# The first MLP's shift vectors: one group moved to VectorE, one held and multiplied on TensorE inside the norm's chain

## The chip, the cores and the metric

The kernel runs on one core of one Trainium2 chip. The metric is the device time of one execution in microseconds (us), as a median of several runs. Below, PE is TensorE's matmul queue, DVE is VectorE, ACT is ScalarE, POOL is GpSimd, and SP is SyncE, whose queue issues nearly all the loads.

## The reference

A trunk of two layers on 256 positions of width 2048. Layer 0 mixes with a causal convolution module (pw1, a gate, a depthwise convolution, a LayerNorm, pw2), layer 1 with a Mamba-2 mixer. An MLP follows each mixer. Every sublayer is normed, and scaled, shifted and gated by vectors that come from one conditioning vector c:

```python
sc = jax.nn.silu(c)
for i in range(DEPTH):
    mod = (sc @ w_mod[i] + b_mod[i])[:, None, :]
    sh1, sc1, g1, sh2, sc2, g2 = jnp.split(mod, 6, axis=-1)
    u = rmsnorm(h, norm_mix_g[i]) * (1 + sc1) + sh1
    ...
    h = h + g1 * mix
    u = rmsnorm(h, norm_mlp_g[i]) * (1 + sc2) + sh2
    h = h + g2 * sq_relu_mlp(u, mlp_w1[i], mlp_w2[i])
return rmsnorm(h, final_norm_g)
```

`sc @ w_mod[i]` is a matrix of 2048 x 12288 times one vector: much to load, little to compute. The change is about sh2, the shift of the first MLP, called SH2 in the code.

## The kernel before

**Modulation columns.** Each of the six vectors of a layer has 16 tiles of 128 outputs. A tile ("column" below) is loaded as 128 x 2048 from `wmT` (1 MB) into a buffer `wm` (two of them) or `hid` (four). Four columns form a group, whose 4 results per partition lie in one small tile `mod<layer><vector><group>`: mod033 is SH2's group 3, mod043 is SC2's, mod023 is G1's. `gemv` multiplies a column in one of two ways. On VectorE it is one instruction (L293) that multiplies the tile by silu(c) and sums it. For groups in `PE_GROUPS` it is four matmuls on TensorE (L284), each of 32 columns, into a PSUM bank from the pool `ms` (two banks); after a group's fourth column ACT copies the bank (L290), and `columns` transposes the copy on TensorE (L305) and reduces it on VectorE (L307). Then GpSimd adds the bias (L321), and for scale vectors applies the norm's weight (L323, L324). All of SH2, groups 0 to 3, is in `PE_GROUPS` before.

**The order of the columns.** `EARLY` lists the columns that are worked between the start of pw1 and the opening of the first MLP; `pump(n)` takes the next n. How many are taken beside each weight tile is written out in tables: `RATE_PW1` for the last four blocks of pw1, `BETWEEN` in the LayerNorm, `RATE_PW2` for the 16 tiles of pw2, `RATE_OPEN` for the 12 tiles of the first MLP's opening.

**The weights.** Each weight tile is 1 MB (four k-tiles of 512 columns), in one of three buffers `w32` (the profile writes `w`). It is split in two halves into a high part `wh` (ACT, L362) and a low part `wl` (VectorE, L364), three buffers of each, so a half is cast as soon as TensorE is done with the half three before it. A tile then takes 48 matmuls (L377): high by high, high by low, low by high. In a name as the profile prints it, `u` is the activation with high and low parts, and `mm` a PSUM bank of the products.

**The stages that matter**, in time order. pw2 runs as `outer` over its blocks 0 to 2 (twelve tiles) and `block` for block 3 (four tiles). Block 3's evacuation (L928) and squares (L567) end the residual. The norm's chain follows: `rstd_cols` sums the squares over partitions on TensorE (L541), ACT takes the root (L546), VectorE the reciprocal (L547) and the diagonal (L516), and TensorE broadcasts it (L521). Then VectorE and ACT make u for the first quarter (`modulate`: nrm L575, high part L505, low part L506), and `outer` starts the first MLP with three blocks together (twelve tiles), quarter by quarter: u for quarter g needs mod03g and mod04g. TensorE's waits in that chain are filled by `turn_over` (L529), matmuls of constants whose result nobody reads, so many as `FILL` says.

**What sets the order on a queue.** A scheduler places each engine's instructions from the program's order, priorities (`high_priority`) and explicit marks (`issue_after`). Loads keep their program order on SP (`stream`, L348). On each engine the instructions then run strictly in their order, each waiting for its semaphores.

Of the kernel before, what the change touches and what calls it, by code (L numbers as in the profile page):

```python
# [15 lines left out]
P = 128  # L16
# [27 lines left out]

RATE_PW1 = [1, 1, 1, 1, 1, 2, 1, 1, 1, 2, 1, 1, 1, 1, 0, 0]
BETWEEN = 5
RATE_PW2 = [1] * 12 + [2, 1, 2, 1]
RATE_OPEN = [1] * 9 + [0] * 3  # L50
RATE_MLP = spread(80, 116) + [0] * 50
RATE_OUT = spread(24, 32)
RATE_LAST = spread(8, 12)
# [12 lines left out]

EARLY = [(0, s, 4 * g + i) for s, g in ((G1, 0), (G1, 1), (G1, 2), (SC2, 0), (SH2, 0), (SH2, 1)) for i in range(4)]
_te = [(0, SH2, 5 + i) for i in range(11)]  # L70
_ve = [(0, G1, 12 + i) for i in range(4)] + [(0, SC2, 4 + i) for i in range(12)]
_mix = _ve[:1]
for _i in range(5):
    _mix += [_te[2 * _i], _ve[1 + _i], _te[2 * _i + 1]]
EARLY = EARLY[:-3] + _mix + _te[10:] + _ve[6:]


PE_GROUPS = {(0, SH2, g) for g in range(4)}
WAIT = 3


# [99 lines left out]
class Trunk:  # L181
    def __init__(self, ctx, nc, tc, a):
        self.nc, self.tc, self.a = nc, tc, a
        pool = lambda n, **kw: ctx.enter_context(tc.tile_pool(name=n, **kw))
        self.one = pool("one", bufs=1)
        self.big = pool("big", bufs=1)
        self.wp = pool("wp", bufs=1)
        self.tp = pool("tp", bufs=2)
        self.mm = pool("mm", bufs=6, space=PSUM)
        self.ms = pool("ms", bufs=2, space=PSUM)  # L190
        self.dr = pool("dr", bufs=1, space=DRAM)
        self.uid = 0
        self.jobs = []
        self.todo = []
        self.ahead = AHEAD
        self.ring, self.rings = 0, ("wm", "hid", "hid")
        self.mod = {}
        self.rows_left = []
        self.spare = 1
        self.act = None  # L200
        self.side = self.mm, "mm"
        self.prologue()
# [61 lines left out]
                                          name=f"mod{layer}{seg}{kg}")  # L264
        return self.mod[key]

    def gemv(self, layer, seg, ct, parts=((0, 4),)):

        nc = self.nc
        self.ring += 1  # L270
        tag = self.rings[self.ring % len(self.rings)]
        w = self.b(tag, [P, D], bufs=4 if tag == "hid" else 2)
        self.stream(w, self.a["wmT"][layer, seg, ct])
        g, i = divmod(ct, 4)
        m = self.mod_tile(layer, seg, g)
        if (layer, seg, g) in PE_GROUPS:
# [185 lines left out]
    def outer(self, srcs, make, evac, pump, there=()):  # L462


        banks = [[self.bank(self.mm, "mm") for _ in range(2)] for _ in srcs]
        self.turn_over(banks[0][0][:, :P], FILL[4] if there else FILL[3], self.pe)
        there = list(there)
        for g in range(4):
            x = make(g)
# [41 lines left out]
    def rstd_bcast(self, sums, n):  # L511

        nc = self.nc
        r = self.rstd_cols(sums, n, FILL[1])
        dg = self.t("diag", [P, 2, P], bufs=1)
        self.dg = nc.vector.tensor_tensor(  # L516
            out=dg, in0=self.ident.rearrange("p (o k) -> p o k", o=1).broadcast_to([P, 2, P]),
            in1=r.rearrange("p (q o) -> p q o", o=1).broadcast_to([P, 2, P]), op=ALU.mult).ins
        ps = self.bank(self.ms, "ms")[:, :T]
        self.turn_over(ps[:, :P], FILL[2], self.pe)  # L520
        self.pe = nc.tensor.matmul(ps, lhsT=self.ones, rhs=dg.rearrange("p q k -> p (q k)"), start=True,  # L521
                                   stop=True).ins
        return ps
# [9 lines left out]
    def rstd_cols(self, sums, n, fill=0):  # L533
# [1 line left out]
        nc = self.nc  # L535
        ps = self.bank(self.ms, "ms")
        if fill:
            self.turn_over(ps[:, :P], fill, self.pe)
        for i, s in enumerate(sums):
            for q in range(2):  # L540
                ins = nc.tensor.matmul(ps[:, q:q + 1], lhsT=s[:, q * P:(q + 1) * P], rhs=self.ones[:, :1],  # L541
# [40 lines left out]
    def conformer(self):  # L582
# [310 lines left out]
        def make(g):  # L893
            if g:
                normed(g)
            if g == 3:
# [3 lines left out]
                for b in range(4):  # L900
# [7 lines left out]
        into = [self.into_h(res, b, gate) for b in range(4)]  # L908
        self.outer([a["pw2"][b] for b in range(3)], make, lambda b, j, parts: into[b](j, parts), pump,
                   there=[(there[0], [half]), (there[1], ()), (there[2], ())])  # L910
        self.block(a["pw2"][3], v, into[3], pump=pump, single=True)
        return res["ss"]


# [498 lines left out]
```

## Time and profile before

| | us |
|---|---|
| median of 3 runs | 2572.73 (2571.45 to 2573.01) |
| the profiled execution's own time | 2573.06 |
| its span, first to last instruction | 2571.3 |
| conformer up to the first product of pw2 | 0 to 313.43 |
| pw2 | 313.43 to 421.03 |
| the norm's chain | 421.03 to 427.59 |
| the first MLP's opening (12 weight tiles) | 427.59 to 497.67 |

The span is what the profile's rows cover; 1.8 us of the execution lie outside it. In a row of a timeline or of the chain stand the start, the length, the engine, the name, the line and a count. One fp32 matmul of the kernel leaves two records of L284, L305, L529 or L541, so four such matmuls show as x8; the products L377 leave one each.

### The profile page before, as it was taken

How to read it: one execution, taken by the hardware profiler on the slowest of the kernel's cores; microseconds unless marked ns; L12 is line 12 of the kernel's file. 1: busy time of each engine (PE TensorE's matmuls, PEld its weight loads, DVE VectorE, ACT ScalarE, POOL GpSimd, SP SyncE). 2: the span in 40 equal slices, each digit the busy share in tenths (PEclk: the TensorE clock that was granted, in tenths of full speed). 3: DMA queues.
4: the chain of work that ended last, by engine and by line, in shares of the span. 5: the costliest groups of instructions: out<-in, count | busy, mean ns of one | idle time of the engine just before them, and what ended most of it. 6: DMA issues, size and time to landing. Idle time of an engine off the chain costs nothing.

```text
span 2571.3 us, 37102 instructions
## 1 busy us (share of the span) xinstructions
PE 2531.0 (98%) x14771; PEld 2181.7 (85%) x14771; DVE 1907.8 (74%) x2460; ACT 1312.3 (51%) x2012; POOL 149.5 (6%) x212
## 2 busy tenths in 40 slices
PE   6999999999999999999999999999999999999998
PEld 5888789988888888888888888888998888888886
DVE  6569567977878878888877777898985565565565
ACT  2068454544434434447767777744454444443443
POOL 0011001000000000000000000000001101101000
PEclk8999999999999999999999999999999999999999
DMA  9998698788888888866555555678765555555553
GB/s 403 368 328 308 252 350 310 283 325 330 313 313 336 310 309 339 313 234 222 198 185 176 174 195 185 240 308 327 297 250 191 197 183 193 197 183 194 196 185 143
DMA packets 94895, 664.85 MB, mean 259 GB/s; under 512 B 10977, under 2 KB 10977, under 8 KB 16769
## 3 DMA queue, kind: packets, MB, share of 16 engines
q1 hardware_dynamic: 89138, 643.87, 67.7%
q0 software_dynamic: 5152, 16.97, 2.3%
q8 instruction: 115, 1.88, 0.3%
q10 hardware_dynamic: 432, 1.66, 0.2%
q14 instruction: 58, 0.48, 0.1%
HBM read 657.02 MB, written 2.20 MB: 256 GB/s over the span
## 4 chain that ended last, share of the span: by engine, by line
PE 94%; DMA 3%; DVE 2%; ACT 1%; issue 0%; POOL 0%; ACTq 0%; SPq 0%; DVEq 0%; POOLq 0%
PE mm L393 48%; PE mm L377 11%; PE mm L447 8%; PE mm L446 8%; PE mm L448 8%; PE mm L743 6%; DMA hid<-wmT 2%; PE mm L689 1%; PE ms L1325 1%; PE ms L743 1%; DMA wm<-wmT 1%; PE ms L284 0%; DVE wl L364 0%; PE ms L541 0%; DVE hid L293 0%
## 5 line engine op out<-in xcount | busy, mean ns | idle before, releaser
L364 DVE TENSOR_TENSOR wl<-w,wh 128x1024 fp32r<-128x1024 f32 x768 | 940.9, 1228 | 487.5 <-ACT wh L362 482.6
L362 ACT CAST wh<-w 128x1024 fp32r<-128x1024 f32 x768 | 806.7, 1051 | 947.4 <-PE mm L393 476.0
L393 PE MATMUL mm<-u,wh 128*128 128x512 f32 x3136 | 994.3, 398 | 0.2 <-ACT wh L362 0.2
L393 PEld LDWEIGHTS mm<-u,wl 128*128 128x128 f32 x3136 | 587.6, 188 | 138.7 <-DVE wl L364 1.3
L393 PE MATMUL mm<-u,wl 128*128 128x256 f32 x3136 | 617.9, 279 | 0.6 <-DVE wl L364 0.6
L393 PEld LDWEIGHTS mm<-u,wh 128*128 128x128 f32 x3136 | 479.9, 189 | 7.7 <-issue 4.3
L446 PE MATMUL mm<-wh,hid 128*128 128x512 f32 x896 | 350.7, 391 | 0.0
L448 PE MATMUL mm<-wh,hid 128*128 128x512 f32 x896 | 348.7, 389 | 0.0
L447 PE MATMUL mm<-wl,hid 128*128 128x512 f32 x896 | 348.7, 389 | 0.0
L293 DVE SCALAR_TENSOR_TENSOR wm<-wm,scb 128x2048 f32<-128x2048 f32 x132 | 301.5, 2284 | 16.9 <-DMA wm<-wmT 16.9
L377 PE MATMUL mm<-u,wh 128*128 128x256 f32 x1408 | 256.0, 284 | 1.6 <-ACT u L505 0.7
L377 PEld LDWEIGHTS mm<-u,wh 128*128 128x128 f32 x1408 | 219.3, 192 | 8.6 <-issue 3.4
L743 PE MATMUL mm<-u,w 128*128 128x256 f32 x864 | 193.3, 385 | 19.6 <-ACT u L617 19.6
L743 PEld LDWEIGHTS mm<-u,w 128*128 128x128 f32 x864 | 165.6, 193 | 46.6 <-ACT u L617 20.8
L377 PE MATMUL mm<-u,wl 128*128 128x256 f32 x704 | 198.6, 283 | 0.0
L446 PEld LDWEIGHTS mm<-wh,hid 128*128 128x128 f32 x896 | 168.2, 188 | 35.6 <-issue 1.0
L447 PEld LDWEIGHTS mm<-wl,hid 128*128 128x128 f32 x896 | 168.2, 188 | 35.2 <-issue 0.5
L448 PEld LDWEIGHTS mm<-wh,hid 128*128 128x128 f32 x896 | 168.2, 188 | 35.1
L393 PE MATMUL mm<-hid,wh 128*128 128x512 f32 x448 | 141.8, 397 | 0.0
L377 PEld LDWEIGHTS mm<-u,wl 128*128 128x128 f32 x704 | 134.7, 192 | 1.7 <-DVE wl L364 0.8
L293 DVE SCALAR_TENSOR_TENSOR hid<-hid,scb 128x2048 f32<-128x2048 f32 x44 | 100.4, 2284 | 43.0 <-DMA hid<-wmT 35.6
L321 POOL TENSOR_TENSOR mod<-mod,par 128x4 f32<-128x4 f32 x46 | 38.0, 826 | 1118.4 <-DVE wm L293 907.8
(263 smaller groups left out, 2029.7 us busy)
## 6 DMA issues: line engine op xcount, KB each, us to landing
w<-w SPq DMA_DIRECT2D x256, 1024.0 KB, 4.9
wm<-wmT SPq DMA_DIRECT2D x139, 1024.0 KB, 7.4
w<-win SPq DMA_DIRECT2D x80, 1024.0 KB, 4.9
hid<-wmT SPq DMA_DIRECT2D x53, 1024.0 KB, 11.1
w<-pw SPq DMA_DIRECT2D x46, 1024.0 KB, 6.8
w<-wout SPq DMA_DIRECT2D x32, 1024.0 KB, 7.2
acc<-ac_d POOLq DMA_DIRECT2D x16, 512.0 KB, 7.5
xpad<-u POOLq DMA_DIRECT2D x24, 131.5 KB, 8.4
```

The lines of the kernel that those rows point to most:

```text
L293: self.sum = nc.vector.scalar_tensor_tensor(out=w, in0=w, scalar=1.0, in1=self.scb, op0=ALU.mult, op1=ALU.mult, accum_out=m[:, i:i + 1]).ins
L321: nc.gpsimd.tensor_tensor(out=m, in0=m, in1=b, op=ALU.add)
L362: nc.scalar.copy(out=wh, in_=w[:, s, :])
L364: nc.vector.tensor_tensor(out=wl, in0=w[:, s, :], in1=wh.bitcast(F32), op=ALU.subtract)
L377: self.pe = self.nc.tensor.matmul(out, lhsT=lhsT, rhs=rhs, skip_group_check=True, **kw).ins
L393: self.pe = self.nc.tensor.matmul(out, lhsT=lhsT, rhs=rhs, start=start and not lows, stop=stop and bool(lows), skip_group_check=True).ins
L446: mm(banks[q], lhsT=hi, rhs=wh[:, k, :], start=g == 0 and t == 0, stop=False)
L447: mm(banks[q], lhsT=hi, rhs=wl[:, k, :], start=False, stop=False)
L448: mm(banks[q], lhsT=lo, rhs=wh[:, k, :], start=False, stop=g == 3 and t == 3)
L689: self.pe = nc.tensor.matmul(o[32 * c:32 * c + 32, :], lhsT=w[:, k, 32 * c:32 * c + 32], rhs=r[:, c, k:k + T], start=k == 0, stop=k == 7, ...
L743: self.pe = nc.tensor.matmul(o, lhsT=w[:, t, j * P:(j + 1) * P], rhs=u[g][:, t, :], start=g == 0 and t == 0 and j < 2, stop=g == 3 and t == 3,
L1325: nc.tensor.matmul(py[64 * f:64 * f + 64, jj * T + q * Q:jj * T + (q + 1) * Q], lhsT=xd[q][:, r, :], rhs=sco[q][:, r, :], start=True, stop ...
```

## The change

It does four things.

- Group 3 of SH2 leaves `PE_GROUPS`: its four columns are now multiplied on VectorE, last of all of `EARLY`.
- Group 2 of SH2 leaves `EARLY`. Its columns (`HELD`) are loaded beside the last two tiles of pw2 and wait in their buffers; `turn` then takes one of them wherever the norm's chain had fillers: one ahead of the sums, one ahead of the broadcast, two ahead of the MLP's products.
- The order of `EARLY` and the rates change. Two columns of G1 are taken beside the last two tiles of pw1 (`RATE_PW1` ends on 1, 1 instead of 0, 0). pw2 takes 13 columns and loads the four held, where it took 18; the opening takes 8 where it took 9.
- `gemv` can be handed a tile that is loaded already; the loading is now `fetch`.

In the changed file the lines of the same code stand 16 to 25 lower: L300 for L284, L321 for L305, L522 for L505, L523 for L506, L538 for L521, L546 for L529, L558 for L541, L592 for L575, L309 for L293, L378 and L380 for L362 and L364, L364 for L348.

```diff
-RATE_PW1 = [1, 1, 1, 1, 1, 2, 1, 1, 1, 2, 1, 1, 1, 1, 0, 0]
+RATE_PW1 = [1, 1, 1, 1, 1, 2, 1, 1, 1, 2, 1, 1, 1, 1, 1, 1]
-RATE_PW2 = [1] * 12 + [2, 1, 2, 1]
-RATE_OPEN = [1] * 9 + [0] * 3
+RATE_PW2 = [1] * 13 + [0] * 3
+RATE_OPEN = [1] * 8 + [0] * 4
...
-EARLY = [(0, s, 4 * g + i) for s, g in ((G1, 0), (G1, 1), (G1, 2), (SC2, 0), (SH2, 0), (SH2, 1)) for i in range(4)]
-_te = [(0, SH2, 5 + i) for i in range(11)]
-_ve = [(0, G1, 12 + i) for i in range(4)] + [(0, SC2, 4 + i) for i in range(12)]
-_mix = _ve[:1]
-for _i in range(5):
-    _mix += [_te[2 * _i], _ve[1 + _i], _te[2 * _i + 1]]
-EARLY = EARLY[:-3] + _mix + _te[10:] + _ve[6:]
-PE_GROUPS = {(0, SH2, g) for g in range(4)}
+EARLY = [(0, s, 4 * g + i) for s, g in ((G1, 0), (G1, 1), (G1, 2), (SC2, 0)) for i in range(4)]
+_te = [(0, SH2, i) for i in range(8)]
+_ve = [(0, s, i) for s, i0 in ((G1, 12), (SC2, 4), (SH2, 12)) for i in range(i0, NT)]
+EARLY += _ve[:2] + _te[:5]
+for _i in range(3):
+    EARLY += [_te[5 + _i], _ve[2 + _i]]
+EARLY += _ve[5:]
+HELD = [(0, SH2, 8 + i) for i in range(4)]
+PE_GROUPS = {(0, SH2, g) for g in range(3)}
...
+    def turn(self, out, n):
+        if self.held:
+            key, w = self.held.pop(0)
+            with self.tc.issue_after(self.pe):
+                self.gemv(*key, w=w)
+        else:
+            self.pe = self.turn_over(out, n, self.pe)
...
-        self.turn_over(banks[0][0][:, :P], FILL[4] if there else FILL[3], self.pe)
+        for _ in range(len(self.held) or 1):
+            self.turn(banks[0][0][:, :P], FILL[4] if there else FILL[3])
...
-        self.turn_over(ps[:, :P], FILL[2], self.pe)
+        self.turn(ps[:, :P], FILL[2])
...
-            self.turn_over(ps[:, :P], fill, self.pe)
+            self.turn(ps[:, :P], fill)
...
-        self.block(a["pw2"][3], v, into[3], pump=pump, single=True)
+        def last(g):
+            if g > 1:
+                for key in HELD[2 * g - 4:2 * g - 2]:
+                    self.held.append((key, self.fetch(*key)))
+            return next(rate)
+        self.block(a["pw2"][3], v, into[3], pump=last, single=True)
```

What this does to the queues, at three places. First TensorE in pw2, with the products between the rows left out. Before, the columns are:

```order
L284 MATMUL ms_1939<-hid_2016,scol 32x512
...
L284 MATMUL ms_1939<-hid_2016,scol 32x512 x3
...
L284 MATMUL ms_1939<-wm_2160,scol 32x512 x4
...
L284 MATMUL ms_1939<-hid_2224,scol 32x512 x4
...
L284 MATMUL ms_2369<-wm_2366,scol 32x512 x4
...
L284 MATMUL ms_2369<-hid_2432,scol 32x512 x4
...
L284 MATMUL ms_2369<-wm_2605,scol 32x512 x4
...
L284 MATMUL ms_2369<-hid_2683,scol 32x512 x4
...
L284 MATMUL ms_2850<-wm_2847,scol 32x512 x4
L284 MATMUL ms_2850<-hid_2855,scol 32x512 x4
...
L284 MATMUL ms_2850<-wm_2986,scol 32x512 x4
L284 MATMUL ms_2850<-hid_2992,scol 32x512 x4
```

In the changed kernel, with the transposes (L321) of the two groups that are done there:

```order
L300 MATMUL ms_1946<-hid_1967,scol 32x512 x4
...
L300 MATMUL ms_1946<-hid_2084,scol 32x512 x4
L321 MATMUL ms_1918<-ident,t_266_1941 128x128 x4
...
L300 MATMUL ms_1946<-wm_2231,scol 32x512 x4
...
L321 MATMUL ms_1946<-ident,t_298_2237 128x128 x4
```

Eleven columns have become three; the first of them now stands behind eight products of the stage instead of 32.

Second, TensorE in the norm's chain, from the last product of pw2 to the first of the MLP. Before:

```order
L377 MATMUL mm_2844<-u_2562,wl_3066 128x256
L529 MATMUL ms_3131<-scb,ones 128x128 x3
L541 MATMUL ms_3131<-ones,ssum_2656 128x1 x2
L541 MATMUL ms_3131<-ones,sq_3111 128x1 x2
L541 MATMUL ms_3131<-ones,sq_3120 128x1 x2
L541 MATMUL ms_3131<-ones,sq_3129 128x1 x2
L529 MATMUL ms_3148<-scb,ones 128x128 x5
L521 MATMUL ms_3148<-diag_3146,ones 128x256
L529 MATMUL mm_3156<-scb,ones 128x128 x6
```

After:

```order
L393 MATMUL mm_2838<-u_2564,wl_3034 128x256
L300 MATMUL ms_3101<-wm_2963,scol 32x512 x4
L558 MATMUL ms_3099<-ones,ssum_2656 128x1 x2
L558 MATMUL ms_3099<-ones,sq_3079 128x1 x2
L558 MATMUL ms_3099<-ones,sq_3088 128x1 x2
L558 MATMUL ms_3099<-ones,sq_3097 128x1 x2
L300 MATMUL ms_3101<-hid_2965,scol 32x512 x4
L538 MATMUL ms_3119<-diag_3117,ones 128x256
L300 MATMUL ms_3101<-hid_3025,scol 32x512 x4
L300 MATMUL ms_3101<-wm_3027,scol 32x512 x4
```

Each run of fillers has become one held column, the last run two. They write the bank ms_3101, which is neither that of the sums nor that of the broadcast.

Third, ACT in the MLP's opening, where u of the fourth quarter is made. The casts (wh) belong, from the top, to the eighth tile (w_468, in the changed kernel w_467), the ninth and the first of the fourth quarter. Before:

```order
L362 CAST wh_3669<-w_468_3660 128x1024
L362 CAST wh_3729<-w_474_3721 128x1024
L362 CAST wh_3733<-w_474_3721 128x1024
L362 CAST wh_3804<-w_485_3802 128x1024
L505 ACTIVATE u_3785<-nrm_3786,mod_2849 128x256
L362 CAST wh_3808<-w_485_3802 128x1024
```

After:

```order
L378 CAST wh_3637<-w_467_3631 128x1024
L378 CAST wh_3641<-w_467_3631 128x1024
L522 ACTIVATE u_3751<-nrm_3752,mod_3434 128x256
L522 ACTIVATE u_3751<-nrm_3756,mod_3434 128x256
L378 CAST wh_3695<-w_473_3693 128x1024
L378 CAST wh_3699<-w_473_3693 128x1024
L522 ACTIVATE u_3751<-nrm_3760,mod_3434 128x256
```

VectorE's rows for the same place, after the change:

```order
L309 SCALAR_TENSOR_TENSOR hid_3572,mod_3434<-hid_3572,scb 128x2048
L592 SCALAR_TENSOR_TENSOR nrm_3752<-h_78,mod_3163,ms_3119 128x256
L592 SCALAR_TENSOR_TENSOR nrm_3756<-h_78,mod_3163,ms_3119 128x256
L380 TENSOR_TENSOR wl_3638<-w_467_3631,wh_3637 128x1024
L380 TENSOR_TENSOR wl_3642<-w_467_3631,wh_3641 128x1024
L309 SCALAR_TENSOR_TENSOR hid_3633,mod_3434<-hid_3633,scb 128x2048
L523 SCALAR_TENSOR_TENSOR u_3751<-nrm_3752,mod_3434,u_3751 128x256
```

mod_3434 is mod033: its last column (L309, the second of the two) stands behind the split of the eighth tile, and the two u that read it stand on ACT ahead of the ninth tile's casts, where before both halves of that tile and one of the next were cast first.

More of the change, by code (lines that the diff above doesn't have):

```diff
@@ L198, in __init__ @@
         self.rows_left = []
+        self.held = []
         self.spare = 1
@@ L265, in mod_tile, with fetch @@
         return self.mod[key]
-    def gemv(self, layer, seg, ct, parts=((0, 4),)):
-        nc = self.nc
+    def fetch(self, layer, seg, ct):
         self.ring += 1
@@ L273, in gemv @@
         self.stream(w, self.a["wmT"][layer, seg, ct])
+        return w
+    def turn(self, out, n):
[5 more added lines that the diff above has]
+            self.pe = self.turn_over(out, n, self.pe)
+    def gemv(self, layer, seg, ct, parts=((0, 4),), w=None):
+        nc = self.nc
+        w = self.fetch(layer, seg, ct) if w is None else w
         g, i = divmod(ct, 4)
```

## The prediction

> **What bounds the kernel now.** I read the first part of the page, then the table of stages, then the chain of work that ended last inside the stretch that the change touches.
>
> ```profile
> span 2571.3 us, 37102 instructions
> PE 2531.0 (98%) x14771; PEld 2181.7 (85%) x14771; DVE 1907.8 (74%) x2460; ACT 1312.3 (51%) x2012; POOL 149.5 (6%) x212
> PE 94%; DMA 3%; DVE 2%; ACT 1%; issue 0%; POOL 0%; ACTq 0%; SPq 0%; DVEq 0%; POOLq 0%
> ```
>
> TensorE (PE) works in 98% of the span and holds 94% of the chain, so a microsecond taken off PE's own queue can be one off the end, as long as nothing else is late there. The average doesn't say where; the stages do. I cut the stretch at the first product of pw2 (313.43), at the first filler of the norm (421.03), at the first product of the first MLP (427.59) and at the end of that MLP's opening (497.67); the first 100 us stand beside them for the DMA, and the end of pw1 (260 to 313.43) for the two columns that move there.
>
> ```profile
> core 0: us, PE busy (x) PEld busy (x) DVE busy (x) ACT busy (x) POOL busy (x), PEclk, DMA share, GB/s
> 0.00:100.00 100.00, 77.11 (x304) 62.04 (x305) 63.11 (x63) 18.39 (x39) 6.33 (x52) 0.90 1.00 409
> 260.00:313.43 53.43, 53.13 (x471) 38.10 (x469) 26.70 (x43) 22.56 (x51) 6.26 (x12) 1.00 0.67 246
> 313.43:421.03 107.60, 107.60 (x870) 96.34 (x871) 76.45 (x98) 54.80 (x86) 2.78 (x5) 1.00 0.90 346
> 421.03:427.59 6.56, 5.50 (x47) 5.18 (x45) 4.14 (x8) 3.37 (x7) 0.00 (x0) 1.00 0.30 105
> 427.59:497.67 70.08, 70.08 (x581) 69.89 (x582) 64.88 (x88) 35.85 (x56) 12.27 (x10) 1.00 0.79 296
> ```
>
> In pw2 PE is busy 107.60 of 107.60 us at full clock, VectorE (DVE) 76.45: whatever leaves PE there is gained. In the norm PE sits in a short chain. In the opening PE is full again, but VectorE is too, nearly: 64.88 of 70.08. That is where the change may have to pay.
>
> **Step 1: pw2 loses eight columns on PE.** "Column" is one 128x2048 tile of a modulation vector. Rows of the chain, then two groups of the same stretch:
>
> ```profile
> 317.97 0.98 PE ms L284 x2
> ...
> 321.53 0.99 PE ms L284 x6
> ...
> 327.99 0.44 PE ms L305 x4
> ...
> 353.82 0.99 PE ms L284 x8
> 354.81 5.95 PE mm L377 x48
> ...
> 361.75 0.59 PE ms L305 x4
> ...
> 393.49 1.85 PE ms L284 x16
> ...
> 401.29 0.44 PE ms L305 x4
> 401.73 5.75 PE mm L377 x48
> ...
> L284 PE MATMUL ms<-hid,scol 128*32 128x512 f32 x48 | 7.4, 600 | 0.0
> ...
> L284 PE MATMUL ms<-wm,scol 128*32 128x512 f32 x40 | 5.3, 604 | 0.0
> ```
>
> A column leaves eight records (L284 x8), so x48 and x40 are 11 columns: six alone at 0.99, two pairs at 1.85, one in two pieces at 0.98 and 0.99. That makes 5.94 + 3.70 + 1.97 = 11.6 us. A weight tile of 48 products takes 5.75 undisturbed and 5.95 behind a column, so each of the ten interruptions drags another 0.20: 2.0 us. Three transposes (L305) are 0.44 + 0.59 + 0.44 = 1.5. Together 15.1. As a cross-check, 16 tiles x 5.75 = 92.0, and 107.6 - 92.0 = 15.6; the 0.5 between the two is PE waiting at the start of the stage, and I leave it. After the change the same stage has three lone columns, 3 x 1.19 = 3.6, and two transposes, 1.0: 4.6 us. The rows therefore give 15.1 - 4.6 = **10.5 us**, and I book **10.0**. The half microsecond is kept back because VectorE gets ten columns here instead of seven.
>
> That is hidden only while VectorE keeps splitting the weights in time:
>
> ```profile
> L364 DVE TENSOR_TENSOR wl<-w,wh 128x1024 fp32r<-128x1024 f32 x32 | 38.9, 1222 | 27.2 <-ACT wh L362 27.1
> ...
> L362 ACT CAST wh<-w 128x1024 fp32r<-128x1024 f32 x32 | 33.3, 1045 | 39.1 <-PE mm L377 39.0
> ...
> L293 DVE SCALAR_TENSOR_TENSOR hid<-hid,scb 128x2048 f32<-128x2048 f32 x6 | 13.7, 2282 | 0.0
> ```
>
> A column on VectorE is 2.28 us, so three more are 6.8. VectorE's idle time there is 107.6 - 76.5 = 31.1; the stage gets 10 us shorter, which leaves about 14 us of idle in 97.6. In time order, the cast of a half tile starts when PE gives up the half three before it, that is two halves or 5.75 us before it is wanted; cast 1.05 and split 1.22 leave 3.5 us. One column (2.28) fits in that, two in a row (4.56) would be 1.1 late. In pw2 the new order always has a split between two columns, so I cost nothing more.
>
> The two G1 columns that move ahead of pw2 cost VectorE 4.6 us at the end of pw1, where it works 26.70 of 53.43, and their transfers pass SP's queue there, between pw1's last tiles and the tap tiles, at a DMA share of 0.67. I book nothing; the bounds are 0 and +2.3, one column that holds up a sum in front of the lifts.
>
> In the DMA, pw2 now moves 346 GB/s x 107.6 = 37.2 MB. It loses one column (17 for 18), so 36.2 MB in 97.6 us: 371 GB/s. The first 100 us ran at 409 with share 1.00, so the queue has room by this trace. The Trainium skill speaks against it: "DMA: Bandwidth & Descriptors", section "Where 436 GB/s comes from", takes about 358 GB/s as a core's share of HBM when both cores of a pair load, and says that this side binds for loads. By that figure the stage would last 101 us and the step would give 6.5 instead of 10; the 409 of the first row differs from it, and since one core runs here the row decides.
>
> **Step 2: the norm's chain with columns for fillers.**
>
> ```profile
> 420.87 0.83 PE L529 MATMUL ms<-scb,ones 128*128 128x128 f32 x6
> 421.54 0.50 PE L541 MATMUL ms<-ones,ssum 128*128 128x1 f32 x4
> 421.90 1.48 PE L541 MATMUL ms<-ones,sq 128*128 128x1 f32 x12
> 423.73 1.38 PE L529 MATMUL ms<-scb,ones 128*128 128x128 f32 x10 [0.35 <-ACT rcol L546]
> 424.95 0.60 PE L521 MATMUL ms<-diag,ones 128*128 128x256 f32 x2
> 425.39 1.50 PE L529 MATMUL mm<-scb,ones 128*128 128x128 f32 x12
> ...
> 423.91 0.04 DVE diag L516
> 423.95 0.31 issue
> 424.25 2.35 DVE wl L364 x2
> 426.61 0.40 DVE nrm L575
> 427.03 0.52 ACT u L505
> 427.59 6.29 PE mm L377 x50
> ```
>
> Now: fillers 0.67, sums 1.70, fillers 1.22, the broadcast 0.44, fillers, and a wait of 0.71 for the first u. The first fillers stand in front of the sums, so a column there (0.99) makes everything behind 0.32 later: diag is ready at 3.5 us into the chain instead of 3.2. The second column writes another bank, needs no wait for rcol, and ends at 0.99 + 1.70 + 0.99 = 3.7; the broadcast starts there, where before it started at 3.9 (424.95). On VectorE one of the two splits that kept nrm waiting (2.35 for both) now stands ahead of the reciprocal, in time that VectorE has free; so nrm comes at about 5.0 instead of 5.6, and u is there at 6.0. PE's own work is 3.7 + 0.44 + 1.85 for the last two columns + 0.20 = 6.2. The chain is then 6.2 against 6.56: I book **-0.3**. Bounds: -0.4, and +0.6 if four columns (3.96) simply replace 3.39 us of fillers end to end. So PE does a whole group in time that it filled before; the copy (L290) of that group goes to ACT between the second and the third u, with the half tile's 2.9 us of products to hide it.
>
> **Step 3: the opening waits for the fourth group.** One transposition more or less stays the same (one before, one after). VectorE has 8 columns for 9. But the last of them now belongs to SH2's group 3, and u of the fourth quarter needs its sum:
>
> ```profile
> 428.37 0.87 DVE L575 SCALAR_TENSOR_TENSOR nrm<-h,mod,ms 128x256 f32<-128x256 f32 x2
> ...
> 428.88 0.91 ACT L505 ACTIVATE u<-nrm,mod 128x256 fp32r<-128x256 f32 x2 [0.94 <-DVE nrm L575]
> ...
> 429.43 0.88 DVE L506 SCALAR_TENSOR_TENSOR u<-nrm,mod,u 128x256 fp32r<-128x256 f32 x2 [0.19 <-ACT u L505]
> ...
> 474.52 1.12 POOL L321 TENSOR_TENSOR mod<-mod,par 128x4 f32<-128x4 f32 x1 [16.17 <-DVE hid L293]
> ```
>
> On ACT the first two u of that quarter now stand ahead of the cast of the ninth tile's first half (half 16); before, they stood behind it. Counting from the first product, with 2.88 us a half and 0.44 for the transposes, half 16 is wanted at 46.5. The cast of half 14 ends at 36.1; VectorE then finishes the u of the quarter before (to 36.6), a column (2.28), two nrm (0.87) and two splits (2.35): 42.1. The last column ends at 44.4, GpSimd's addition (1.12) at 45.5, two u on ACT (0.91) at 46.4, the cast at 47.4 and the split at 48.6. PE's first product of that half waits 0.9; its third, which needs the split, would come at 47.8 and waits 0.8 more. Laid end to end like this the rows overstate a little: I book **+1.5**. Bounds: 0, since the order before met waits for the same quarter with PE full, and +3.5, a column and a split later still (2.28 + 1.22).
>
> **The sum.** -10.0 - 0.3 + 1.5 = -8.8. The profiled execution took 2573.06, so 2564.3; the median before is 0.33 lower than that execution, so **2564.0**. Behind the opening PE is full, and every queue has the order that it had, so I let the 8.8 reach the end.
>
> **Rivals.**
> A, transfers pace pw2. For it: share 0.90 already, and 371 GB/s wanted. Against: 409 in the first row. If the stage stays at its 346, it lasts 36.2 / 0.346 = 104.6 and gives 3.0: about 2571. Chance 0.08. (By the 358 of the Trainium skill's page above it would be 2567.5.)
> B, the held columns don't do what is meant: they land late, or the chain takes them in full. The last one is issued right behind the last tile of pw2, whose buffer comes free some 2.5 tiles (14 us) before the stage ends, and hid lands with a median of 9.2 us:
>
> ```profile
> hid<-wmT SPq DMA_DIRECT2D x12, 1024.0 KB, 9.2
> ```
>
> Against it is that margin of 5. If it happened, the chain would be 2 to 4 us longer: 2566 to 2568. Chance 0.08.
> C, VectorE becomes the bound of the opening and the fourth group costs two columns rather than a wait: +4 instead of +1.5, 2566.5 to 2568. 64.88 of 70.08 busy speaks for it, one column fewer against. Chance 0.08.
> D, slower: in pw2 every column on VectorE pushes the next split behind PE's need by its whole 2.28. Ten of them are 22.8, less the 10.0: about 2586. It decides from the point where VectorE's wait for the casts (27.1 us over 32 splits) is used up; the sum above leaves 14. Chance 0.04.
> The forecast, 2562 to 2566, has 0.72.
>
> **How the numbers follow.** 2572.73 - 0.2% is 2567.6, and a measurement of this kernel tells no less than that from no change. Faster by more: the forecast, and some two thirds of B and C and a third of A: 0.85. Within 0.2%: the rest of A, B and C: 0.11. Slower: D, 0.04. The range: at the low end 10.5 with a chain at -0.4 and no wait in the opening, 2561.8, rounded to 2561.5; at the high end B and C and the better half of A, 2568.5.
>
> **What would show it.** Right: pw2 at about 97.5 us with PE full and three columns of eight records; the norm at 6.2 to 6.6 with four; a wait of PE of 1 to 2 us for a split some 46 us into the opening, behind u of the fourth quarter; everything later shifted alike. Wrong: PE idle in pw2 behind L364 (D) or casts waiting for DMA (A), a chain over 7 us (B), more than 3 us of idle in the opening (C). I should also be wrong if the stretch before 313 grew through the two moved columns.

## The result, and the profile after

| | us |
|---|---|
| before, median of 4 runs | 2572.87 (2571.45 to 2574.26) |
| changed, median of 4 runs | 2561.74 (2561.14 to 2562.01) |
| ratio, with its 95% interval | 0.996 (0.9948 to 0.9971) |
| forecast | 2564.0 (2561.5 to 2568.5) |

The changed kernel is 11.1 us faster; the forecast was 8.8. First the page's head and the table of stages of the changed kernel, cut at the same events as before: the first product of pw2, the first matmul behind its last product, the first product of the MLP, and the first product behind its opening.

```profile
span 2559.8 us, 36983 instructions
PE 2518.8 (98%) x14707; PEld 2175.6 (85%) x14707; DVE 1916.5 (75%) x2467; ACT 1312.7 (51%) x2011; POOL 146.9 (6%) x212
...
core 0: us, PE busy (x) PEld busy (x) DVE busy (x) ACT busy (x) POOL busy (x), PEclk, DMA share, GB/s
260.00:311.64 51.64, 50.83 (x459) 36.49 (x458) 28.43 (x41) 22.71 (x51) 6.27 (x12) 1.00 0.83 299
311.64:408.57 96.93, 96.93 (x801) 93.72 (x801) 81.22 (x102) 52.46 (x83) 7.48 (x10) 1.00 0.89 348
408.57:415.07 6.50, 6.39 (x52) 2.89 (x51) 4.72 (x9) 3.69 (x7) 0.00 (x0) 1.00 0.79 272
415.07:485.63 70.56, 69.94 (x584) 69.74 (x581) 62.98 (x84) 36.30 (x56) 4.72 (x5) 1.00 0.74 280
```

The kernel before, cut exactly at the same events (the prediction's cuts lie 0.16 later at the chain and 0.17 later at the end of the opening):

```profile
313.43:420.87 107.44, 107.44 (x868) 96.18 (x869) 76.45 (x98) 54.65 (x85) 2.78 (x5) 1.00 0.90 346
420.87:427.59 6.72, 5.66 (x48) 5.34 (x46) 4.14 (x8) 3.52 (x7) 0.00 (x0) 1.00 0.31 113
427.59:497.50 69.91, 69.91 (x580) 69.72 (x581) 64.71 (x86) 35.76 (x55) 12.27 (x10) 1.00 0.79 296
```

| stage | before | after | moved | booked |
|---|---|---|---|---|
| up to the first product of pw2 | 313.43 | 311.64 | -1.79 | 0 |
| pw2 | 107.44 | 96.93 | -10.51 | -10.0 |
| the norm's chain | 6.72 | 6.50 | -0.22 | -0.3 |
| the MLP's opening | 69.91 | 70.56 | +0.65 | +1.5 |
| all behind it, to the last product | 2061.94 | 2062.33 | +0.39 | 0 |

TensorE is busy 96.93 of 96.93 us in pw2, with three columns where there were eleven, and VectorE's 81.22 still leaves it 15.7 idle. The last row is the same TensorE instructions in the same order in both; over the fourteen profiles of this study that stretch takes 2060.8 to 2062.3 in eleven and 2063.8 to 2065.9 in three, and nothing is read from it.

The first row needs a look of its own, since the two programs are the same up to that point but for two columns near its end. Windows of 3.41 us around TensorE's wait for the third quarter of u in pw1 (the kernel before, then the changed one; PEclk is the granted clock):

```profile
94.55:97.96 3.41, 0.84 (x5) 0.48 (x4) 2.56 (x4) 0.99 (x3) 0.20 (x1) 1.00 1.02 423
97.96:101.37 3.41, 3.41 (x10) 2.69 (x10) 3.41 (x4) 0.82 (x2) 0.00 (x0) 0.50 1.01 420
```

```profile
95.02:98.43 3.41, 1.75 (x8) 1.52 (x9) 2.56 (x5) 1.82 (x4) 0.20 (x1) 1.00 1.02 423
98.43:101.84 3.41, 3.41 (x18) 3.00 (x17) 3.41 (x3) 0.00 (x0) 0.00 (x0) 1.00 1.01 420
```

In the kernel before, TensorE worked 0.84 of 3.41 us in one window, and in the next it ran at half clock: 10 products instead of 18, so 1.7 us lost. In the changed kernel the same wait fell across two windows, TensorE worked 1.75 us in the emptier one, and the clock stayed. Of the -1.79, then, -1.7 is this window, -0.70 an earlier start of that quarter (96.68 for 97.38), and +0.58 a wait further on, for a DMA in front of a convolution of pw1, that this execution of the kernel before does not have:

```profile
277.81 3.67 PE L706 MATMUL mm<-xpad,acc 128*32 128x256 f32 x64 [0.51 <-DMA xpad<-u]
```

Whether any of the three belongs to the change is what part of the experiments is for.

### The profile page after: what moved, and what is told of

Read it like the earlier page. It is cut to its first block, busy times and chain, and to the rows that moved or that the text cites. A ratio compares the mean times of both kernels' runs of the same rounds, so it can differ in the third digit from the quotient of the medians.

```text
span 2559.8 us, 36983 instructions
## 1 busy us (share of the span) xinstructions
PE 2518.8 (98%) x14707; PEld 2175.6 (85%) x14707; DVE 1916.5 (75%) x2467; ACT 1312.7 (51%) x2011; POOL 146.9 (6%) x212
## 5 line engine op out<-in xcount | busy, mean ns | idle before, releaser
L380 DVE TENSOR_TENSOR wl<-w,wh 128x1024 fp32r<-128x1024 f32 x768 | 940.9, 1229 | 472.6 <-ACT wh L378 468.2
L378 ACT CAST wh<-w 128x1024 fp32r<-128x1024 f32 x768 | 808.2, 1053 | 935.4 <-PE mm L409 478.5
L309 DVE SCALAR_TENSOR_TENSOR wm<-wm,scb 128x2048 f32<-128x2048 f32 x133 | 303.9, 2285 | 17.9 <-DMA wm<-wmT 17.9
L393 PE MATMUL mm<-u,wh 128*128 128x256 f32 x1408 | 254.7, 284 | 0.9 <-DVE u L523 0.6
L393 PEld LDWEIGHTS mm<-u,wh 128*128 128x128 f32 x1408 | 219.2, 192 | 4.0 <-ACT u L519 1.3
L393 PE MATMUL mm<-u,wl 128*128 128x256 f32 x704 | 198.0, 283 | 0.6 <-DVE wl L380 0.6
L309 DVE SCALAR_TENSOR_TENSOR hid<-hid,scb 128x2048 f32<-128x2048 f32 x47 | 107.3, 2286 | 40.8 <-DMA hid<-wmT 40.7
L393 PEld LDWEIGHTS mm<-u,wl 128*128 128x128 f32 x704 | 134.6, 192 | 0.8 <-DVE wl L380 0.8
L409 PEld LDWEIGHTS mm<-hid,wl 128*128 128x128 f32 x448 | 84.2, 188 | 19.8
```

The lines of the kernel that those rows point to most:

```text
L309: self.sum = nc.vector.scalar_tensor_tensor(out=w, in0=w, scalar=1.0, in1=self.scb, op0=ALU.mult, op1=ALU.mult, accum_out=m[:, i:i + 1]).ins
L378: nc.scalar.copy(out=wh, in_=w[:, s, :])
L380: nc.vector.tensor_tensor(out=wl, in0=w[:, s, :], in1=wh.bitcast(F32), op=ALU.subtract)
L393: self.pe = self.nc.tensor.matmul(out, lhsT=lhsT, rhs=rhs, skip_group_check=True, **kw).ins
L409: self.pe = self.nc.tensor.matmul(out, lhsT=lhsT, rhs=rhs, start=start and not lows, stop=stop and bool(lows), skip_group_check=True).ins
```

## The experiments

Each is a variant of the changed kernel (of the kernel before where it says so), timed beside the kernel before on the same chip.

**hold_off: group 2 back in pw2, fillers back in the chain.**

```diff
-RATE_PW2 = [1] * 13 + [0] * 3
+RATE_PW2 = [1] * 6 + [2] + [1] * 9
...
-_te = [(0, SH2, i) for i in range(8)]
+_te = [(0, SH2, i) for i in range(12)]
...
-HELD = [(0, SH2, 8 + i) for i in range(4)]
+HELD = []
```

> The changed kernel, but SH2's group 2 is multiplied by TensorE in pw2 again (seven columns there instead of three) and the norm's chain has its fillers back. Theory (holding is worth the four columns' price in pw2, because the chain takes them in time it spent on fillers: 6.50 us with columns, 6.56 with fillers): pw2 grows from 96.9 us by 4 x 1.19 + 0.44 for one more transposition = 5.2, the chain by 0.1, so about 5 us over the changed kernel's 2561.7, 2566.5 to 2567. Rival 1 (the held columns only moved the price, some of it shows up behind the chain): 2 to 3 us, 2564. Rival 2 (the whole gain is group 3's on VectorE and the start of the program): no difference, 2561.7. Start: the profile of the kernel before has a window of 3.41 us at half clock at 98 us, that of the changed kernel has none; if that is chance, it comes and goes over these runs whatever the variant.

Measured: 2564.11 (2563.59 to 2566.01), before 2571.99, the first rival's figure. But the seven times lie in two groups, 2563.6 to 2564.1 and 2565.3 to 2566.0, and the profile, of 2566, has a half-clock window at 98 us. So the comparison with 2561.7 can't be read to better than two microseconds, and the run was made again with that wait filled (hold_fill, below).

**g3_tensor: group 3 back on TensorE in pw2, group 2 still held.**

```diff
-_te = [(0, SH2, i) for i in range(8)]
-_ve = [(0, s, i) for s, i0 in ((G1, 12), (SC2, 4), (SH2, 12)) for i in range(i0, NT)]
+_te = [(0, SH2, i) for i in (*range(8), *range(12, NT))]
+_ve = [(0, s, i) for s, i0 in ((G1, 12), (SC2, 4)) for i in range(i0, NT)]
...
-PE_GROUPS = {(0, SH2, g) for g in range(3)}
+PE_GROUPS = {(0, SH2, g) for g in range(4)}
```

> The changed kernel, but SH2's group 3 is multiplied by TensorE in pw2 again (seven columns there), group 2 stays held; VectorE has six columns instead of ten in pw2 and SC2's group 3 is the last in the opening. Theory (a column that leaves TensorE in pw2 is worth 1.19 whoever takes it, as long as VectorE has room): pw2 +4.8 to +5.2, and the wait of 0.62 us in the opening for the fourth quarter goes, so +4.2 to +4.6: about 2566.1. Rival 1 (VectorE's ten columns cost pw2 or the opening something that the profile spreads out): less than +3.5, under 2565.2. Rival 2 (moving group 3 gains nothing, the hold gained all): 2561.7.

Measured: 2566.19 (2565.27 to 2567.05), 4.5 over the changed kernel; the theory said 2566.1. Its stages pw2, chain and opening:

```profile
312.25:414.34 102.09, 102.08 (x836) 94.99 (x836) 74.73 (x96) 53.72 (x85) 5.24 (x8) 1.00 0.86 338
414.34:420.84 6.50, 6.39 (x51) 2.89 (x50) 3.80 (x8) 3.78 (x7) 0.00 (x0) 1.00 0.56 173
420.84:490.95 70.11, 69.94 (x585) 69.74 (x582) 63.08 (x85) 35.86 (x55) 8.09 (x7) 1.00 0.77 278
```

pw2 is 5.16 longer and the opening 0.45 shorter. Four columns on TensorE cost pw2 5.2 us; the same four on VectorE cost nothing in pw2 and 0.45 in the opening.

**two_late: the two columns of G1 back in pw2** (twelve on VectorE there).

```diff
-RATE_PW1 = [1, 1, 1, 1, 1, 2, 1, 1, 1, 2, 1, 1, 1, 1, 1, 1]
+RATE_PW1 = [1, 1, 1, 1, 1, 2, 1, 1, 1, 2, 1, 1, 1, 1, 0, 0]
...
-RATE_PW2 = [1] * 13 + [0] * 3
+RATE_PW2 = [1] * 15 + [0]
...
```

> The changed kernel, but the two columns of G1 go back from pw1's last two tiles into pw2, where VectorE then has twelve columns instead of ten. Theory (their transfers make the padded copy of u land 0.51 us late in front of a convolution at 277.8 us, and pw2 has room for two columns on VectorE): the start of pw2 comes 0.5 earlier, pw2 keeps its 96.9, so 2561.2, same within the measurement. Rival 1 (VectorE in pw2 is at its limit and each further column pushes the splits by its 2.28): +4.6, 2566. Rival 2 (the 0.51 was chance): 2561.7.

Measured: 2561.28 (2560.70 to 2565.42). The wait in front of the convolution is absent and pw2 starts at 311.07, 0.57 earlier; but pw2 lasts 97.57 instead of 96.93, because its first column on TensorE now waits for its load:

```profile
313.08 1.06 PE L300 MATMUL ms<-wm,scol 128*32 128x512 f32 x8 [0.57 <-DMA wm<-wmT]
```

In this execution the half microsecond only changes its place. That the two columns cause the wait in front of the convolution is not shown: the kernel before has it in before_fill (0.3), and among the variants that take the two columns early it runs from none (g1_mid) to 0.93 (hold_fill). Moving the two columns is worth nothing that can be told here, and twelve columns on VectorE do not break pw2.

**before_gap and before_fill: the kernel before, with matmuls that add zero in TensorE's wait at 95 us.**

```diff
             for g in range(3):
+                if g == 2:
+                    with self.tc.issue_after(self.pe):
+                        for _ in range(2):
+                            nc.tensor.matmul(banks[0][0][:32, :], lhsT=vpad[0][:, :1].broadcast_to([P, 32]),
+                                             rhs=self.scb[:, :512], start=False, stop=False, skip_group_check=True)
                 for i in range(n):
```

(before_gap had eight of them a quarter later.)

> The kernel before, with eight matmuls that add zero to a bank put into TensorE's wait of 2.57 us for the first u of the last quarter of pw1's opening (at 95 us of the profile). Nothing else differs. Theory (1.7 us of the 11.1 between the two kernels are a window of 3.41 us at half clock that follows this wait in the kernel before and not in the changed one, and have nothing to do with the change): no half-clock window at 98 us, pw2 starts about 1.7 earlier, 1 to 1.7 us faster than the kernel before in the runs in which that one has the window: about 2571.2 against 2572.9. Rival (the change itself makes the start of the program faster, or the window costs nothing): 2572.9, no difference.

Measured for before_gap: 2580.69 (2579.13 to 2583.62), 8.7 slower. The place was wrong: its eight matmuls ran at 124.8, behind the third quarter, where TensorE waited for nothing, and took 7.05 us there. It says nothing on the clock.

> before_gap filled the wrong place (its matmuls stood behind the wait, took 7 us and said nothing on the clock). Here two matmuls that add zero, 0.88 us each, stand in front of the third quarter's first products in pw1's opening, in TensorE's wait of 2.0 to 2.6 us at 95 us; else it is the kernel before. Theory (the times of the kernel before fall in two groups, 2571.0 to 2572.1 and 2572.4 to 2573.6, because a window of 3.41 us at half clock at 98 us follows that wait in some executions): no half-clock window in the profile, and all times in the lower group, 2571 to 2572. Rival (the two groups have another cause): both groups again, or a time above both because the matmuls cost 1.8.

Measured for before_fill: 2570.65, eleven runs from 2570.15 to 2571.65; the sixteen runs of the kernel before beside it spread from 2569.96 to 2573.31 with a median of 2572.39, six of them at 2571.26 or below and ten at 2572.15 or above. The upper group is gone. Its windows at that place:

```profile
94.50:98.00 3.50, 3.31 (x11) 1.28 (x11) 2.65 (x5) 1.47 (x4) 0.20 (x1) 1.00 1.02 424
98.00:101.40 3.40, 3.40 (x18) 2.99 (x17) 3.40 (x3) 0.34 (x1) 0.00 (x0) 1.00 1.02 422
```

Of the nine profiles whose wait at 95 us is open (1.8 to 2.6 us long), four have the half-clock window behind it: the kernel before, hold_off, g1_late and open_early. Of the five with the wait filled, none has. The nine divide by the emptiest of the 3.41 us windows around the wait: with 0.84 to 1.39 us of TensorE's work in it the next one ran at half clock (the four), with 1.58 to 2.15 it did not (the five). So up to 1.7 us of the first comparison are chance and not the change: the profiled execution of the kernel before has the window, and the changed kernel's four times lie too close together (2561.14 to 2562.01) for one among them to have it and another not. The earlier start of the quarter isn't the change's either, as far as these profiles show: the kernel before starts it at 96.94 and 96.96 in before_fill and before_gap, the changed kernel and its variants at 96.63 to 97.17.

**after_fill: the changed kernel with the same two matmuls.**

> The changed kernel with the same two matmuls in the wait at 95 us that before_fill has, so that neither has a half-clock window there. Theory (with that chance taken out, the change is worth what the stages differ by between 260 us and the end of the opening: 0.58 - 10.5 - 0.2 + 0.65 = -9.5): 2570.65 - 9.5 = 2561.2, in one group of times. Rival (the 11.1 us between the first medians are all the change's): 2570.65 - 11.1 = 2559.5.

Measured: 2560.49 (2559.99 to 2563.09), before 2572.17. Against before_fill that is -10.2, between the two expectations and nearer to the theory's -9.5. The 0.6 between them is explained by a term of that theory: the +0.58 at the end of pw1 came from the first pair of profiles, and in this pair it isn't there. Both wait in front of the convolution (0.3 before, 0.2 after), and pw2 starts at the same time, in before_fill and then in after_fill:

```profile
311.63 0.51 PE L377 MATMUL mm<-u,wh 128*128 128x256 f32 x2 [0.30 <-ACT u L502]
```

```profile
311.59 0.50 PE L393 MATMUL mm<-u,wh 128*128 128x256 f32 x2 [0.29 <-ACT u L519]
```

With -0.04 in place of +0.58 the stages give -0.04 - 10.51 - 0.22 + 0.65 = -10.1. The chain and the opening in this sum are those of the first pair, since the profile of before_fill has another half-clock window, in the norm's chain (7.19 us instead of 6.72).

**hold_fill: hold_off with the two matmuls.**

> hold_off with the two zero matmuls at 95 us, so that it can be set against after_fill (2560.5) without the half-clock window that hold_off had in part of its executions. Theory (holding gives back pw2's 5.0 us less 0.9 that the chain with fillers is shorter and 0.4 in the opening): 3.7 us over after_fill, 2564.2. Rival 1 (the columns are free in the chain): 5.0, 2565.5. Rival 2 (their gain is 2.4, what the lower group of hold_off's times is over the changed kernel): 2562.9.

Measured: 2564.54 (2563.44 to 2565.45), 4.05 over after_fill; the theory said 3.7. With each set against the kernel before on its own chip (2571.80 here, 2572.17 for after_fill) it is 4.4, so the medians alone do not tell 3.7 from the first rival's 5.0; the stages do. Its stages, and the chain's rows with the fillers:

```profile
312.04:413.99 101.95, 101.95 (x836) 94.99 (x837) 82.86 (x104) 53.67 (x84) 8.68 (x11) 1.00 0.90 348
413.99:419.58 5.59, 5.56 (x48) 5.32 (x46) 3.41 (x8) 3.52 (x7) 0.00 (x0) 1.00 0.10 40
419.58:489.71 70.13, 69.48 (x577) 69.28 (x577) 63.37 (x84) 35.39 (x55) 5.41 (x4) 1.00 0.77 283
```

```profile
414.00 0.83 PE L546 MATMUL ms<-scb,ones 128*128 128x128 f32 x6
...
417.04 0.42 DVE L533 TENSOR_TENSOR diag<-ident,rcol 128x256 f32<-128x256 f32 x1
417.38 1.22 DVE L380 TENSOR_TENSOR wl<-w,wh 128x1024 fp32r<-128x1024 f32 x1
...
418.51 0.86 DVE L592 SCALAR_TENSOR_TENSOR nrm<-h,mod,ms 128x256 f32<-128x256 f32 x2
419.02 0.91 ACT L522 ACTIVATE u<-nrm,mod 128x256 fp32r<-128x256 f32 x2 [1.28 <-DVE nrm L592]
```

With fillers the chain now takes 5.59, not 6.72: only one split (1.22) stands between diag and nrm, where the kernel before had two (2.35). Holding the columns is worth 5.02 in pw2, less 0.91 in the chain and 0.4 in the opening: 3.7.

**open_early: one column a tile sooner, so that group 3's sum comes earlier.**

```diff
-RATE_PW2 = [1] * 13 + [0] * 3
-RATE_OPEN = [1] * 8 + [0] * 4
+RATE_PW2 = [1] * 14 + [0] * 2
+RATE_OPEN = [1] * 7 + [0] * 5
```

> The changed kernel with one column taken beside pw2's fourteenth tile instead of the opening's eighth, so that SH2's last group is complete a tile earlier in the opening. Theory (TensorE's wait of 0.62 us in the opening, at 463 us, is the wait for that group's sum, and pw2 hides an eleventh column): the wait goes, the opening shrinks from 70.6 to 69.9, pw2 stays at 96.9: -0.6, 2561.1. Rival 1 (the wait only moves to the next quarter or to pw2): 2561.7. Rival 2 (an eleventh column breaks pw2): +2, 2563.7.

Measured: 2564.33 (2563.20 to 2565.53). Part of it is the half-clock window that its profile has at 98 us; pw2 keeps its 96.93, but the opening grows to 72.18. What the products' line (L393) waited for in the opening, in open_early and then in the changed kernel (us, times; matmuls and weight loads both count):

```profile
  DVE wl L380: 2.6, 5
```

```profile
  DVE wl L380: 1.4, 2
```

The wait did not go, it came some 4 us sooner: the two u that need the sum stand on ACT in front of the next tile's casts here too, and three more records wait for splits. The first rival is right, with a loss besides.

**g1_vector, g1_late, g1_mid, g1_13: group 1 to VectorE as well**, so that pw2 keeps no column on TensorE. They differ in how many columns VectorE has beside pw2's tiles (13, 16, 14, 13; the last of the 16 runs in the norm's chain) and in what stands ahead of pw2.

```diff
-_te = [(0, SH2, i) for i in range(8)]
-_ve = [(0, s, i) for s, i0 in ((G1, 12), (SC2, 4), (SH2, 12)) for i in range(i0, NT)]
...
+_te = [(0, SH2, i) for i in range(4)]
+_ve = [(0, s, i) for s, i0, i1 in ((G1, 12, NT), (SC2, 4, 8), (SH2, 4, 8), (SC2, 8, NT), (SH2, 12, NT)) for i in range(i0, i1)]
...
-PE_GROUPS = {(0, SH2, g) for g in range(3)}
+PE_GROUPS = {(0, SH2, g) for g in (0, 2)}
```

> The changed kernel, but SH2's group 1 goes to VectorE too: none of SH2 is left on TensorE in pw2, VectorE has thirteen columns there (29.6 us) instead of ten. Theory (pw2 has room on VectorE: 81.2 busy of 96.9 us now, so 88 of 93 then, and every column that leaves TensorE gives 1.19): pw2 shorter by 3 x 1.19 + 0.44 = 4.0, so about 92.9 long and 2557.7 for the kernel. Rival (each VectorE column beyond the room pushes a split by 2.28; the room is used up at some 11 columns): pw2 keeps 96 to 97 us or grows, 2561 to 2564, with waits of TensorE for wl in pw2.

Measured: 2563.44 (2561.25 to 2564.08), 1.7 slower than the changed kernel. No wait for a split in pw2, yet pw2 lasts 95.50. The windows around its start:

```profile
308.85:312.26 3.41, 1.38 (x13) 1.18 (x11) 3.38 (x7) 0.95 (x3) 0.00 (x0) 1.00 1.01 423
312.26:319.08 6.82, 6.22 (x29) 6.22 (x30) 5.06 (x8) 5.70 (x11) 0.00 (x0) 0.50 0.25 71
```

One of the columns had landed on VectorE in front of the LayerNorm's reciprocal; TensorE waited 2.64 us for the first u of pw2 and then ran 6.8 us at half clock, 3.1 of them work lost inside pw2. Neither theory had this. Without it pw2 would be some 92.4, an estimate from these rows: the thirteen columns were hidden.

> As g1_vector, and the two columns of G1 and one more go into pw2 as well: sixteen columns on VectorE there (36.5 us), one beside every tile, the last of them in front of the norm's chain. VectorE would be busy 81.2 + 6 x 2.28 = 95 us in a stage that would last 93. Theory (the room ends here): VectorE bounds pw2, TensorE waits there for 2 to 5 us, and the chain grows by up to 2.3 for the column that stands in front of the reciprocal: 3 to 7 us slower than g1_vector, 2561 to 2565. Rival (the room isn't what counts, columns are hidden whatever their number): as g1_vector, 2557.7.

Measured: 2559.74 (2558.73 to 2564.50), 3.7 faster than g1_vector where 3 to 7 slower was expected: the theory fell. With fifteen columns inside pw2 and VectorE at 91 of 94.5 us, TensorE waits for a split once there (the profile is of the slowest of the five executions; its half-clock windows, at 97.5, 411.6 and 1193.2 us, lie outside pw2):

```profile
PE mm L390 <- DVE wl L377: 0.7, 1, 0.7
```

g1_mid and g1_13 take the column out of the LayerNorm (`BETWEEN = 4`), add five fillers ahead of pw2 (13 instead of 8) and the two zero matmuls; g1_13 puts one column beside a tile of pw1 that g1_mid leaves to pw2.

> The changed kernel with SH2's group 1 on VectorE as in g1_vector, but without its fault: the column of 2.28 us that stood on VectorE in front of the LayerNorm's reciprocal goes into pw2 (fourteen columns on VectorE there), TensorE has five more fillers ahead of pw2 (0.86 us less of wait, 13 instead of 8) and the two zero matmuls at 95 us. Theory (g1_vector lost 1.2 us of pw2's start to that column and 3.4 us to 6.83 us at half clock that followed TensorE's wait of 2.64; VectorE's room in pw2 reaches to fourteen columns): pw2 starts at 311 without a half-clock window and lasts 92 to 93, so 4 to 5 us less than the changed kernel: 2557. Rival (VectorE's fourteen columns, 90.4 us of 93, bound pw2): waits for wl in pw2 of 2 us and more, 2559 to 2561.

Measured: 2559.59 (2559.14 to 2561.73), the rival's figure. pw2 takes 95.74, and TensorE waits in three places, each time for the split that stands right behind a column (in front of that column stand an addition of the LayerNorm, a second column, and the evacuation of a block):

```profile
PE mm L390 <- DVE wl L377: 1.3, 3, 0.5
```

> As g1_mid, but with thirteen columns on VectorE in pw2; the fourteenth goes beside one of pw1's last tiles. Theory (thirteen columns are hidden, as in g1_vector, whose half tiles in pw2 all took 2.88 us once the clock was back; g1_mid lost 2 us to three waits of 0.6 to 0.7 for a split that stood behind a column and another split): pw2 92.2 to 93.5 instead of 95.7, the chain 6.5, the start of pw2 at 311 to 311.7, no half-clock window: about 2557. Rival (VectorE at 88 us of 93 waits whatever the order): pw2 95 and 2559 to 2560, no better than g1_mid.

Measured: **2557.94** (2556.91 to 2558.57), ratio to the kernel before 0.9942 (0.9929 to 0.9956): the best of the study, 3.8 under the changed kernel, 2.6 under after_fill, which has the same two zero matmuls, and nearer to the theory's 2557 than to the rival's 2559 to 2560. No wait for a split is left in pw2, but the clock drops in the chain:

```profile
312.09:405.69 93.60, 93.48 (x772) 92.80 (x772) 86.97 (x107) 51.59 (x82) 10.76 (x10) 1.00 0.91 362
405.69:413.83 8.14, 8.03 (x52) 3.07 (x51) 4.40 (x10) 3.86 (x7) 0.00 (x0) 0.79 0.55 203
413.83:483.48 69.65, 69.65 (x585) 69.65 (x582) 62.93 (x83) 36.36 (x56) 0.90 (x5) 1.00 0.79 285
```

pw2 is 3.33 shorter than in the changed kernel, where the count of columns gives 4.0: the first 48 products take 6.69 us here and 7.25 there with a column of 0.99 among them, so that column had in part filled a wait. At a PEclk of 0.79 the chain is 8.14 instead of 6.50. How much of that is to be had is open: g1_mid, with a chain of 6.50 and the same last columns, waits in the opening again (70.92 instead of 69.65), and chain and opening together take 77.79 here, 77.42 in g1_mid and 77.06 in the changed kernel.

## Why the prediction was right, and where its sizes were off

**pw2** (booked -10.0, measured -10.51). The rows gave 10.5, and 10.5 it was: 1.19 for each lone column, its 0.99 and the 0.20 that the products behind it lose, held in both directions (g3_tensor +5.16 for four columns with a transposition). The half microsecond kept back for VectorE was not needed.

**VectorE's room in pw2.** The conclusion held, the reason only in part. By the sum of idle time there was room for ten columns; the runs show that the sum isn't what decides. Fifteen columns gave one wait, fourteen gave three, thirteen none. The second argument of that step, that two columns in a row in front of a split come 1.1 late, isn't enough either: such a pair had no wait behind it in two_late (at 396.5 us), g1_late (365.3) and g1_13 (364.7), and cost 0.47 in g1_mid (366.1) and, with a short sum between the two, 0.67 in g1_late (395.8). How far VectorE is ahead when the row begins must count as well; that is argued from these rows, and no run varies it alone.

**The end of pw1** (booked 0 within 0 to +2.3; +0.58 in the first pair of profiles, -0.04 in the filled pair). No sum on VectorE held up the lifts. The half microsecond of the first pair is a DMA that the kernel before waits for as well once it gets there as early, so the 0 held.

**The chain** (booked -0.3, measured -0.22). The size was right and the account incomplete. These are the rows of the changed kernel:

```profile
408.57 1.06 PE L300 MATMUL ms<-wm,scol 128*32 128x512 f32 x8
...
409.56 0.61 PE L558 MATMUL ms<-ones,ssum 128*128 128x1 f32 x4
...
411.44 1.07 PE L300 MATMUL ms<-hid,scol 128*32 128x512 f32 x8
...
412.04 0.42 DVE L533 TENSOR_TENSOR diag<-ident,rcol 128x256 f32<-128x256 f32 x1
412.39 1.22 DVE L380 TENSOR_TENSOR wl<-w,wh 128x1024 fp32r<-128x1024 f32 x1
412.61 0.67 PE L538 MATMUL ms<-diag,ones 128*128 128x256 f32 x2
413.21 1.06 PE L300 MATMUL ms<-hid,scol 128*32 128x512 f32 x8
413.52 0.87 DVE L592 SCALAR_TENSOR_TENSOR nrm<-h,mod,ms 128x256 f32<-128x256 f32 x2
...
414.03 0.91 ACT L522 ACTIVATE u<-nrm,mod 128x256 fp32r<-128x256 f32 x2 [2.22 <-DVE nrm L592]
414.10 1.04 PE L300 MATMUL ms<-wm,scol 128*32 128x512 f32 x8
```

diag starts 3.47 into the chain (forecast 3.5), nrm 4.95 (5.0), u is there at about 6.0 (6.0). Only the broadcast waits for the end of diag, at 4.04 and not at 3.7, and behind it two columns on TensorE end at 6.50 and not at 6.2. Two effects make up the -0.22: one split less in front of nrm gives 1.13 (6.72 to 5.59, hold_fill), and the columns cost 0.91 of it. "A whole group in time that it filled before" was therefore too kind: of what the group cost in pw2, 5.0, some 3.7 are gained (hold_fill, with the opening's 0.4).

**The opening** (booked +1.5, measured +0.65). The mechanism was the one named: u of the fourth quarter stands on ACT ahead of the ninth tile's cast and waits for group 3's last column.

```profile
456.96 2.28 DVE L309 SCALAR_TENSOR_TENSOR hid<-hid,scb 128x2048 f32<-128x2048 f32 x1
459.18 0.08 DVE L309 DVE_READ_ACCUMULATOR hid<-hid,scb 128x1 f32 x1
459.33 0.20 POOL L337 TENSOR_TENSOR mod<-mod,par 128x4 f32<-128x4 f32 x1 [17.27 <-DVE hid L309]
459.57 0.91 ACT L522 ACTIVATE u<-nrm,mod 128x256 fp32r<-128x256 f32 x2 [5.37 <-POOL mod L337]
...
460.39 1.99 ACT L378 CAST wh<-w 128x1024 fp32r<-128x1024 f32 x2
...
461.70 2.35 DVE L380 TENSOR_TENSOR wl<-w,wh 128x1024 fp32r<-128x1024 f32 x2
...
462.97 0.39 PE L393 MATMUL mm<-u,wl 128*128 128x256 f32 x1 [0.62 <-DVE wl L380]
```

Counted from the first product (415.07), the column ends at 44.2 (forecast 44.4), u at 45.4 (46.4), the cast starts there. The microsecond lies in one term: GpSimd's addition took 0.20 where 1.12 had been taken over from the row of the kernel before. TensorE then waits 0.62 once, for the split, not 0.9 for the cast as well. g1_13 and g1_late have no wait in the opening (69.65), but both stand behind a chain of 8.1 us, which gives VectorE 1.6 us more; behind 6.50, g1_mid with the same last columns waits. That this order can do without the wait is therefore not shown.

**Together.** -8.8 less the 0.5 kept back, less 0.85 in the opening, plus 0.08 in the chain is -10.1; with the wait at 95 us filled in both kernels the difference measured is -10.2. The sum was thus 1.3 to 1.4 too small by its own terms. The 0.9 more of the first comparison is likely the half-clock window, which the profiled execution of the kernel before, from which the sum started, happened to have; how it divides is not shown, since with the fill the medians of both kernels fell, by 2.2 and 1.25. The measured 2561.74 lies only 0.24 above the low end of the range, and that chance has its part in it.

**The rivals.** A, transfers: pw2 moved 348 GB/s, not the 371 expected, and did not suffer: TensorE waited for no load there, and the queue carried part of its bytes earlier and later: 299 GB/s instead of 246 up to pw2, 272 instead of 113 in the chain. B, the held columns: landed in time, no wait in front of any of them. C, VectorE in the opening: one wait of 0.62. D, VectorE in pw2: not with ten columns, and in g1_mid, at fourteen, as three waits and not as a whole column each.

## What to carry to other kernels

Price a piece of work on a full engine by its own time and by what its neighbours lose behind it, and expect to get that back when it goes, less what it had filled of a wait; the same work put into a wait is not free, so measure the wait's chain once with the old filling, or its shortening is credited to the wrong edit. Room on a second engine is not its idle share: look at the row of its instructions in front of the one that is waited for, and at how far ahead the engine is when that row begins. A term read from one pair of profiles, as the 0.58 here, is looked for in a second pair before it is charged to the change. And look at the granted clock, window by window, before two executions are compared: here a wait of 2.0 us cost 1.7 more behind it (hold_off), and one of 2.64 cost 3.1 (g1_vector).

## What the runs showed of the hardware

**The clock.** Half-clock stretches came in whole windows of 3.41 us (6.82 in g1_vector), at places that change from one execution to the next; in the kernel before they begin at 22.86 and at 97.96 us, 22 windows apart. At the wait at 95 us, windows with 0.84 to 1.39 us of TensorE's work were followed by one; windows with 1.58 to 2.15 were not. The Trainium skill, "TensorE: Matmul & The Clock Gate", section "What's actually happening", has a free-running window of 3413 ns and two states, half and full, and the rows agree. Its section "Why this matters for your kernels" advises against waits longer than about 3 us; here waits of 2.0 to 2.6 us were enough in four of nine profiles, and the measurement decides. In the chain of g1_13 TensorE's records fill 4.40 of the 4.51 us ahead of the half-clock window, so records that look busy need not hold the clock.

**GpSimd beside VectorE.** The addition of a 128x4 tile (0.20 us in the rows above) takes 1.12 where a split runs on VectorE, and ends when the split does. Two rows of the kernel before:

```profile
474.36 1.22 DVE L364 TENSOR_TENSOR wl<-w,wh 128x1024 fp32r<-128x1024 f32 x1
474.52 1.12 POOL L321 TENSOR_TENSOR mod<-mod,par 128x4 f32<-128x4 f32 x1 [16.17 <-DVE hid L293]
```

The Trainium skill, "GPSIMD Engine Reference", section "Key points", says that GpSimd shares its SBUF interfaces with VectorE and contends with instructions of two SBUF inputs, which the split is; the trace agrees. A duration of GpSimd is therefore read with what VectorE does beside it, which step 3 of the prediction left out.

**Small matmuls.** A column's four matmuls of 32 columns each go to four different groups of 32 columns of the array and take 0.99 us together; the eight of before_gap, all into the same group, took 0.88 each.
